# An expert-parallel two-layer network: from unrolled, framework-ordered instructions to one section with hand-set semaphores and a looping TensorE

## The chip, the cores and the metric

The kernel runs on one core of one Trainium2 chip. The metric is device time in microseconds, the median of several runs. Times inside a run come from the hardware profiler's trace, whose span runs from the first to the last instruction of the core.

## The reference

Eight experts, each with 256 rows of 512 values, a hidden width of 2048 and its own two weight matrices:

```python
n_experts, capacity, hidden, expert_hidden = 8, 256, 512, 2048
x  = randn(8, 256, 512);  w1 = randn(8, 512, 2048);  w2 = randn(8, 2048, 512)   # all float32
h   = np.matmul(x, w1)
h   = np.maximum(h, 0)
out = np.matmul(h, w2).astype(np.float32)
```

Each weight matrix of one expert has 4 MB in float32, so w1 and w2 together are 64 MB that are read once. The input x and the output have 4 MB each.

## The kernel before

The weights are loaded by GpSimd's DMA queue, which turns float32 into bf16 on the way. The loads are made for pairs of experts (8 MB a load), and for the last pair one expert at a time, the last w2 in two halves. On the chip there is room for four experts of w1 and four of w2 (two buffers of a pair each). x is loaded into the place of a later w2 pair, transposed by TensorE into xT, and copied out by VectorE and ScalarE in turns.

A first layer (`layer1`) makes 16 column blocks of h, four matmuls each, two blocks to a psum buffer; ScalarE applies the ReLU into hT. A second layer (`layer2`) makes two row blocks of the output, 16 matmuls each. The framework (Tile) sets the semaphores; the order of TensorE's and GpSimd's instructions is that of the program text.

```python
psum_t = ...(name="psum_t", bufs=2)     # transposes
psum_h = ...(name="psum_h", bufs=3)     # first layer
psum_o = ...(name="psum_o", bufs=3)     # second layer
hT_pool = ...(name="hT_pool", bufs=2)

def layer1(e):
    hT = hT_pool.tile([P, K2, C], BF16, name="hT")
    for pr in range(K2 // 2):                          # 8 groups
        h_ps = psum_h.tile([P, 2, C], FP32, name="h_ps")
        for s in range(2):
            j = pr * 2 + s
            for ko in range(K1):                       # 4 matmuls of 256 columns
                nc.tensor.matmul(h_ps[:, s, :], w1_r[:, ko, :, j], xT[:, ko, :, e, :],
                                 start=(ko == 0), stop=(ko == K1 - 1))
        nc.scalar.activation(hT[:, pr*2:pr*2+2, :]..., h_ps[:]..., Relu)
    return hT

def layer2(e, hT):
    # 32 matmuls of 512 columns; order (m, k), for the last expert (k, m)
    ...
            nc.vector.tensor_copy(out_sb[:, e, m, :], o_ps[m][:])
    # last expert: one of its two copies on ScalarE, both into out_last
```

The first layers of a pair come ahead of both second layers, except for the last pair, whose weights are loaded one expert at a time:

```python
for i, g in enumerate(GROUPS):                         # (0,1) (2,3) (4,5) (6,7)
    issue(i + B, i + B)                                # loads whose buffer is free by then
    whole = len(g) > 1 and (g,) in W1_LOADS            # true for the first three pairs
    if whole:
        hs = [layer1(e) for e in g]
        issue(i + 1 + B, i + B)
    else:
        hs = [None] * len(g)
    for e, hT in zip(g, hs):
        layer2(e, hT or layer1(e))
        if e == 5:
            ...; store_first(); ...                    # a small store, then the last half of w2
        if e == E - 2:
            store()                                    # experts 0 to 6, 3.5 MB
nc.sync.dma_start(out_v[:, E - 1, :], out_last[:]...)  # expert 7, 512 KB
```

Of the kernel before, what the change touches and what calls it, by code (L numbers as in the profile page):

```python
# [1 line left out]

# [5 lines left out]

FP32 = mybir.dt.float32  # L10
BF16 = mybir.dt.bfloat16


@with_exitstack
def kernel(
    ctx: ExitStack,
    tc: tile.TileContext,
    x: bass.AP,
    w1: bass.AP,
    w2: bass.AP,  # L20
    out: bass.AP,
):
    nc = tc.nc
    P = 128
    E, C, H = x.shape
    F = w1.shape[2]
    MC = C // P
    K1 = H // P
    K2 = F // P

    R = E * C // P

    x_v = x.rearrange("e (pp r) k -> (e pp) (r k)", r=R)
    w1_v = w1.rearrange("e (p ko) n -> p e (ko n)", ko=K1)
    w2_v = w2.rearrange("e (p j) n -> p e (j n)", p=P)
    out_v = out.rearrange("e (p mo) k -> p e (mo k)", mo=MC)

    GROUPS = [(0, 1), (2, 3), (4, 5), (6, 7)]
    W1_LOADS = [(g,) for g in GROUPS[:-1]] + [((6,),), ((7,),)]
    W2_LOADS = [(g, 0, K2) for g in GROUPS[:-1]] + [((6,), 0, K2), ((7,), 0, 8), ((7,), 8, K2)]
    NG = max(len(g) for g in GROUPS)
    GROUP = {e: g for g in GROUPS for e in g}

    const = ctx.enter_context(tc.tile_pool(name="const", bufs=1))
    w1_pool = ctx.enter_context(tc.tile_pool(name="w1_pool", bufs=4 // NG))  # L50
    w2_pool = ctx.enter_context(tc.tile_pool(name="w2_pool", bufs=4 // NG))
    hT_pool = ctx.enter_context(tc.tile_pool(name="hT_pool", bufs=2))
    psum_t = ctx.enter_context(tc.tile_pool(name="psum_t", bufs=2, space=bass.MemoryType.PSUM))
    psum_h = ctx.enter_context(tc.tile_pool(name="psum_h", bufs=3, space=bass.MemoryType.PSUM))
    psum_o = ctx.enter_context(tc.tile_pool(name="psum_o", bufs=3, space=bass.MemoryType.PSUM))

    identity = const.tile([P, P], BF16, name="identity")
    xT = const.tile([P, K1, MC, E, P], BF16, name="xT")
    out_sb = const.tile([P, E - 1, MC, H], FP32, name="out_sb")
    out_last = const.tile([P, MC, H], FP32, name="out_last")  # L60

    HEAD = 4
    x_head = const.tile([P, HEAD * H], FP32, name="x_head")
    x_sb = w2_pool.tile([P, NG, K2 * H], BF16, name="w2_sb")[:, 0, :]

    w1t, w2t = {}, {}

    def load_x():
        nc.gpsimd.dma_start(x_sb[:, HEAD * H:], x_v[:, HEAD * H:])  # L69

    def load_w1(es):
        g = GROUP[es[0]]
        if es[0] == g[0]:
            w1t[g] = w1_pool.tile([P, NG, K1 * F], BF16, name="w1_sb")
        i = es[0] - g[0]
        nc.gpsimd.dma_start(w1t[g][:, i:i + len(es), :], w1_v[:, es[0]:es[-1] + 1, :])  # L76

    def load_w2(es, a, b):
        g = GROUP[es[0]]
        if es[0] == g[0] and a == 0:  # L80
            w2t[g] = w2_pool.tile([P, NG, K2 * H], BF16, name="w2_sb")
        i = es[0] - g[0]
        nc.gpsimd.dma_start(  # L83
            w2t[g][:, i:i + len(es), a * H:b * H],
            w2_v[:, es[0]:es[-1] + 1, a * H:b * H],
        )

    def store_first():


        nc.gpsimd.dma_start(  # L91
            out_v[:16, 0:5:2, :16], out_sb[:16, 0:5:2, 0, :16]
        )

    def store():
        nc.gpsimd.dma_start(  # L96
            out_v[:, :E - 1, :], out_sb[:].rearrange("p e m h -> p e (m h)")
        )

    def transpose_x():  # L100


        x_r = x_sb.rearrange("p (r2 m q ko) -> p r2 m q ko", m=MC, q=P, ko=K1)
        for i, (ko, m) in enumerate((ko, m) for ko in range(K1) for m in range(MC)):
            ps = psum_t.tile([P, R // MC, P], BF16, name="xt_ps")
            for r2 in range(R // MC):
                nc.tensor.transpose(ps[:, r2, :], x_r[:, r2, m, :, ko], identity[:])  # L107
            src = ps[:].rearrange("k r2 ep -> k ep r2")
            dst = xT[:, ko, m].rearrange("k e (pp r2) -> k (e pp) r2", r2=R // MC)
            if i % 2:  # L110
                nc.scalar.copy(dst, src)  # L111
            else:
                nc.vector.tensor_copy(dst, src)  # L113

    def layer1(e):
        g = GROUP[e]
        w1_r = w1t[g][:, e - g[0], :].rearrange("p (ko q j) -> p ko q j", ko=K1, j=K2)
        hT = hT_pool.tile([P, K2, C], BF16, name="hT")
        for pr in range(K2 // 2):
            h_ps = psum_h.tile([P, 2, C], FP32, name="h_ps")  # L120
            for s in range(2):
                j = pr * 2 + s
                for ko in range(K1):
                    nc.tensor.matmul(  # L124
                        h_ps[:, s, :],
                        w1_r[:, ko, :, j],
                        xT[:, ko, :, e, :],
                        start=(ko == 0),
                        stop=(ko == K1 - 1),
                    )  # L130
            nc.scalar.activation(  # L131
                hT[:, pr * 2:pr * 2 + 2, :].rearrange("p a c -> p (a c)"),
                h_ps[:].rearrange("p a c -> p (a c)"),
                mybir.ActivationFunctionType.Relu,
            )
        return hT

    def layer2(e, hT):
        g = GROUP[e]
        last = e == E - 1  # L140
        o_ps = [psum_o.tile([P, H], FP32, name="o_ps") for _ in range(MC)]
        if last:
            order = [(k, m) for k in range(K2) for m in range(MC)]
        else:
            order = [(k, m) for m in range(MC) for k in range(K2)]
        for k, m in order:
            nc.tensor.matmul(  # L147
                o_ps[m][:],
                hT[:, k, m * P:(m + 1) * P],
                w2t[g][:, e - g[0], k * H:(k + 1) * H],  # L150
                start=(k == 0),
                stop=(k == K2 - 1),
            )
            if k == K2 - 1:
                if last and m == 1:
                    nc.scalar.copy(out_last[:, m, :], o_ps[m][:])  # L156
                elif last:
                    nc.vector.tensor_copy(out_last[:, m, :], o_ps[m][:])  # L158
                else:
                    nc.vector.tensor_copy(out_sb[:, e, m, :], o_ps[m][:])  # L160

    loads = []
    for i, g in enumerate(GROUPS):
        own = [(load_w1, l) for l in W1_LOADS if l[0][0] in g]
        own += [(load_w2, l) for l in W2_LOADS if l[0][0] in g]
        own.sort(key=lambda f: (f[1][0][0], f[0] is load_w2))
        loads += [(i, *f) for f in own]
    tail = loads.pop()  # L170

    def issue(ready1, ready2):

        while loads:
            i, f, l = loads[0]
            if i >= (ready1 if f is load_w1 else ready2):
                break
            loads.pop(0)
            f(*l)

    B = 4 // NG
    nc.sync.dma_start(x_head[:], x_v[:, :HEAD * H])
    nc.vector.tensor_copy(x_sb[:, :HEAD * H], x_head[:])  # L183
    with tc.manual_schedule(engines={mybir.EngineType.PE, mybir.EngineType.Pool}):
        load_x()
        make_identity(nc, identity)
        issue(B, B - 1)
        transpose_x()
        for i, g in enumerate(GROUPS):
            issue(i + B, i + B)  # L190
            whole = len(g) > 1 and (g,) in W1_LOADS
            if whole:
                hs = [layer1(e) for e in g]
                issue(i + 1 + B, i + B)
            else:
                hs = [None] * len(g)
            for e, hT in zip(g, hs):
                layer2(e, hT or layer1(e))
                if e == 5:
                    issue(E, E)  # L200
                    store_first()
                    loads.append(tail)
                    issue(E, E)
                if e == E - 2:
                    store()
    nc.sync.dma_start(out_v[:, E - 1, :], out_last[:].rearrange("p m h -> p (m h)"))

# [1 line left out]
_INS = ['x', 'w1', 'w2']  # L209
# [26 lines left out]
```

## Time and profile before

| | |
|---|---|
| time, median of 3 runs | 181.32 us (181.3 to 181.46) |
| span of the profiled run | 179.7 us, 1827 instructions |
| TensorE busy, matmuls | 127.1 us (71%), 824 |
| ScalarE busy | 44.1 us (25%) |
| VectorE busy | 16.5 us (9%) |
| GpSimd busy | 9.9 us (6%) |
| moved by DMA | 40.48 MB written at the far end, mean 225 GB/s |
| read from HBM | 71.30 MB |
| mean granted TensorE clock | 0.930 |

The page divides the span into 40 slices and gives for each the busy share of every engine in tenths. The chain of work that ended last is followed back from the last instruction, at each step to what released it. "another core or an unknown queue" in it stands for a load whose end the chain could not name; where TensorE waits in that way before a layer, the wait ends with the landing of that layer's weights. Durations of matmuls in the trace overlap, so the time of a layer is read from the start of its first matmul to the start of the next layer. GB/s counts what is written, which for weights is bf16, half of what is read.

### The profile page before, as it was taken

What the parts mean: (1) busy time and instruction counts of PE and PEld (TensorE: products, weight loads), DVE (VectorE), ACT (ScalarE), POOL (GpSimd) and SP (SyncE); (2) the same over time, 40 slices, a digit from 0 to 9 for tenths busy, and PEclk for the clock granted to TensorE, in tenths of its full rate; (3) what the DMA queues carried; (4) which work ended last, traced back from release to release, by engine and by line L of the source; (5) the groups of instructions that cost most, each with busy time, mean ns of one, the idle gap of its engine ahead of it and who ended that gap; (6) DMA issues with size and microseconds to landing.
All of it is one profiled execution on the core that took longest, in us unless ns stands there. A gap on an engine that the chain in (4) does not pass through costs nothing.

```text
span 179.7 us, 1827 instructions
## 1 busy us (share of the span) xinstructions
PE 127.1 (71%) x824; PEld 90.5 (50%) x832; DVE 16.5 (9%) x20; ACT 44.1 (25%) x70; POOL 9.9 (6%) x20
## 2 busy tenths in 40 slices
PE   0017600899629991999569943999199999999960
PEld 0017500699514440899434412999034479469520
DVE  0205500000001111000002210000002210110010
ACT  2004400266500000266500000566100026116210
POOL 7000100000100001000100030000002000002000
PEclk9999975699978999699999997899969999999998
DMA  6999998999999899999999999999999999999995
GB/s 201 252 219 204 233 230 186 226 233 208 201 233 230 190 222 233 208 201 233 230 193 219 233 208 201 233 230 193 219 233 204 204 233 228 195 210 214 349 420 217
DMA packets 3735, 40.48 MB, mean 225 GB/s; under 512 B 272, under 2 KB 272, under 8 KB 1296
## 3 DMA queue, kind: packets, MB, share of 16 engines
q0 software_dynamic: 3440, 38.80, 96.8%
q1 hardware_dynamic: 288, 1.57, 2.4%
q8 instruction: 6, 0.10, 0.2%
q14 instruction: 1, 0.01, 0.0%
HBM read 71.30 MB, written 4.20 MB: 420 GB/s over the span
## 4 chain that ended last, share of the span: by engine, by line
PE 58%; DMA 27%; another core or an unknown queue 9%; POOL 1%; issue 1%; ACT 0%; POOLq 0%
PE o_ps L147 32%; DMA w_sb<-in_w_dram 27%; PE h_ps L124 25%; POOL w_sb L76 0%; POOL w_sb L69 0%; ACT out_last L156 0%; POOL identity masks.py:199 0%; POOL identity masks.py:197 0%; POOLq masks.py:199 0%; POOLq L220 0%
## 5 line engine op out<-in xcount | busy, mean ns | idle before, releaser
L124 PE MATMUL h_ps<-xT,w_sb 128*128 128x256 bf16 x512 | 61.3, 285 | 20.2 <-DMA w_sb<-in_w_dram 20.2
L124 PEld LDWEIGHTS <-w_sb 128*128 128x128 bf16 x512 | 58.3, 146 | 24.1 <-DMA w_sb<-in_w_dram 21.9
L147 PE MATMUL o_ps<-w_sb,hT 128*128 128x512 bf16 x248 | 58.6, 393 | 12.8 <-DMA w_sb<-in_w_dram 12.2
L131 ACT ACTIVATE hT<-h_ps 128x512 bf16<-128x512 f32 x64 | 38.2, 597 | 106.8 <-PE h_ps L124 106.8
L147 PEld LDWEIGHTS <-hT 128*128 128x128 bf16 x256 | 25.6, 101 | 44.3 <-issue 9.3
L160 DVE COPY out_sb<-o_ps 128x512 f32<-128x512 f32 x14 | 9.7, 692 | 128.7 <-PE o_ps L147 128.7
L107 PE MATMUL xt_ps<-identity,w_sb 128*128 128x128 bf16 x64 | 7.7, 309 | 13.8 <-DVE w_sb L183 6.9
L107 PEld LDWEIGHTS <-w_sb 128*128 128x128 bf16 x64 | 6.7, 145 | 14.6 <-DVE w_sb L183 6.9
L111 ACT COPY xT<-xt_ps 128x1024 bf16<-128x1024 bf16 x4 | 4.0, 1012 | 16.5 <-PE xt_ps L107 16.5
L83 POOL DMA_DIRECT2D w_sb<-in_w_dram x6 | 3.8, 637 | 53.6 <-PE o_ps L147 36.5
L113 DVE COPY xT<-xt_ps 128x1024 bf16<-128x1024 bf16 x4 | 4.9, 1224 | 10.2 <-PE xt_ps L107 10.2
L76 POOL DMA_DIRECT2D w_sb<-in_w_dram x5 | 3.3, 658 | 44.6 <-PE h_ps L124 44.6
L96 POOL DMA_DIRECT2D out_dram<-out_sb x1 | 1.0, 968 | 27.3 <-issue 27.3
L91 POOL DMA_DIRECT2D out_dram<-out_sb x1 | 0.6, 554 | 29.2 <-DVE out_sb L160 29.2
L156 ACT COPY out_last<-o_ps 128x512 f32<-128x512 f32 x1 | 0.6, 585 | 6.3 <-PE o_ps L147 6.3
L158 DVE COPY out_last<-o_ps 128x512 f32<-128x512 f32 x1 | 0.7, 692 | 13.4 <-PE o_ps L147 13.4
L183 DVE CAST w_sb<-x_head 128x2048 bf16<-128x2048 f32 x1 | 1.2, 1228 | 5.6 <-DMA x_head<-in_x_dram 5.6
L111 ACT ACT_TABLE_LOAD x1 | 1.3, 1283 | 0.7 <-PEq L220 0.7
L69 POOL DMA_DIRECT2D w_sb<-in_x_dram x1 | 0.7, 679 | 0.8 <-POOLq L220 0.8
masks.py:199 POOL TENSOR_SCALAR_AFFINE_SELECT identity<-identity 128x128 bf16<-128x128 bf16 x1 | 0.3, 287 | 0.1
masks.py:197 POOL MEMSET identity<- 128x128 bf16 x1 | 0.2, 223 | 0.0
L220 POOL MEMSET const-float32-0.0<- 128x1 f32 x1 | 0.1, 93 | 0.2 <-issue 0.2
(3 smaller groups left out, 0.3 us busy)
## 6 DMA issues: line engine op xcount, KB each, us to landing
w_sb<-in_w_dram POOLq DMA_DIRECT2D x6, 4096.0 KB, 62.1
w_sb<-in_w_dram POOLq DMA_DIRECT2D x3, 2048.0 KB, 51.5
out_dram<-out_sb POOLq DMA_DIRECT2D x1, 3584.0 KB, 12.9
w_sb<-in_w_dram POOLq DMA_DIRECT2D x2, 1024.0 KB, 44.7
w_sb<-in_x_dram POOLq DMA_DIRECT2D x1, 1536.0 KB, 11.6
x_head<-in_x_dram SPq DMA_DIRECT2D x1, 1024.0 KB, 4.8
out_dram<-out_last SPq DMA_DIRECT2D x1, 512.0 KB, 4.3
out_dram<-out_sb POOLq DMA_DIRECT2D x1, 3.0 KB, 27.8
```

Of the source, the lines that this page charges most:

```text
L69: nc.gpsimd.dma_start(x_sb[:, HEAD * H:], x_v[:, HEAD * H:])
L76: nc.gpsimd.dma_start(w1t[g][:, i:i + len(es), :], w1_v[:, es[0]:es[-1] + 1, :])
L83: nc.gpsimd.dma_start(w2t[g][:, i:i + len(es), a * H:b * H], w2_v[:, es[0]:es[-1] + 1, a * H:b * H],)
L96: nc.gpsimd.dma_start(out_v[:, :E - 1, :], out_sb[:].rearrange("p e m h -> p e (m h)"))
L107: nc.tensor.transpose(ps[:, r2, :], x_r[:, r2, m, :, ko], identity[:])
L111: nc.scalar.copy(dst, src)
L113: nc.vector.tensor_copy(dst, src)
L124: nc.tensor.matmul(h_ps[:, s, :], w1_r[:, ko, :, j], xT[:, ko, :, e, :], start=(ko == 0), stop=(ko == K1 - 1),)
L131: nc.scalar.activation(hT[:, pr * 2:pr * 2 + 2, :].rearrange("p a c -> p (a c)"), h_ps[:].rearrange("p a c -> p (a c)"), mybir.ActivationF ...
L147: nc.tensor.matmul(o_ps[m][:], hT[:, k, m * P:(m + 1) * P], w2t[g][:, e - g[0], k * H:(k + 1) * H], start=(k == 0), stop=(k == K2 - 1),)
L160: nc.vector.tensor_copy(out_sb[:, e, m, :], o_ps[m][:])
L183: nc.vector.tensor_copy(x_sb[:, :HEAD * H], x_head[:])
```

## The change

All of the work goes into one section in which each engine has its own program text, and every wait is a semaphore set by hand. TensorE's program becomes loops: one over the four values of ko for the transposes, one over the experts, and inside it one over blocks of four column blocks of F. The addresses of weights and xT come from registers there. The aim is a short TensorE program whose order and waits are all explicit.

The parts that matter, with cuts marked by "...":

```diff
-    psum_h = ctx.enter_context(tc.tile_pool(name="psum_h", bufs=3, space=bass.MemoryType.PSUM))
-    psum_o = ctx.enter_context(tc.tile_pool(name="psum_o", bufs=3, space=bass.MemoryType.PSUM))
+    NS = 4
+    GJ = 2
+    UG = 2
+    NG = K2 // GJ
...
+    w1_sb = nc.alloc_sbuf_tensor("w1_sb", [P, NS, K1 * F], BF16)
+    w2_sb = nc.alloc_sbuf_tensor("w2_sb", [P, NS, K2 * H], BF16)
+    hT = nc.alloc_sbuf_tensor("hT", [P, K2, C], BF16)
+    h_ps = [nc.alloc_psum_tensor(f"h_ps{i}", [P, GJ * C], FP32) for i in range(UG)]
+    o_ps = [nc.alloc_psum_tensor(f"o_ps{i}", [P, H], FP32) for i in range(MC)]
...
+    with tc.tile_critical(no_gpsimd_drain=True):
+        sp = nc.sync
...
+        for i, (w, e, n, a, b) in enumerate(loads):       # same loads, same order
+            sp.wait_ge(d_w[i], 16)
+            if w == 1:
+                sp.sem_inc(c_w1, n)
             else:
+                sp.sem_inc(c_w2, 2 * n * b // K2)
...
+        for i, (w, e, n, a, b) in enumerate(loads):       # GpSimd
+            old = e + n - 1 - NS
+            if w == 2 and e == 2:
+                pool.wait_ge(p_xt, K1 * MC)
+            if old >= 0:
+                if w == 1:
+                    pool.wait_ge(p_h, NG * (old + 1))
+                else:
+                    pool.wait_ge(p_o, MC * (old + 1))
...
+            for g in range(NG):                           # ScalarE, for each e
+                act.wait_ge(p_h, e * NG + g + 1)
+                act.activation(hT[...], h_ps[g % UG][:], Relu).then_inc(c_h)
...
+        def take(s, n):
+            pe.wait_ge(s, n).then_inc(s, -n)
...
+        with nc.Fori(0, E, 1, engines=[PE]) as e:
+            ring = pe.snap((e % NS) * (K1 * F))
+            col = pe.snap(e * P)
+            take(c_w1, 1)
+            with nc.Fori(0, NG // UG, 1, engines=[PE]) as u:
+                first = pe.snap(ring + u * (UG * GJ))
+                for g in range(UG):
+                    take(c_h, 1)
+                    for i in range(GJ):
+                        for ko in range(K1):
+                            c = first + (ko * F + g * GJ + i)
+                            mm = pe.matmul(
+                                h_ps[g][:, i * C:(i + 1) * C],
+                                w1_f[:, bass.DynSlice(c, P, step=K2)],
+                                xT[:, ko, :, bass.ds(col, P)],
+                                start=(ko == 0), stop=(ko == K1 - 1),
+                            )
+                    mm.then_inc(p_h)
+            take(c_o, MC)
+            for k in range(K2):
+                if k % (K2 // 2) == 0:
+                    take(c_w2, 1)
+                late = k - (K2 - UG * GJ)
+                if late >= 0 and late % GJ == 0:
+                    pe.wait_ge(c_h, late // GJ + 1)
+                for m in range(MC):
+                    mm = pe.matmul(
+                        o_ps[m][:], hT[:, k, m * P:(m + 1) * P],
+                        w2_f[:, bass.ds(ring + k * H, H)],
+                        start=(k == 0), stop=(k == K2 - 1),
+                    )
+                    if k == K2 - 1:
+                        mm.then_inc(p_o)
```

A `take` waits until a semaphore has a value and lowers it by that much. Sync waits for each load and passes the news on to TensorE by raising `c_w1` or `c_w2`. There is one hT, so ScalarE waits for the second layer of expert e - 1 before the first ReLU of expert e. The two copies of the last expert and its store stay as they were; the small store and the 3.5 MB store are issued by GpSimd at the same places of its queue.

## The prediction

> **What bounds the kernel now.** I read three views of the kernel before: the DMA row and queue table of the page, then the chain of work that ended last, then stretches of the span cut at the points where the chain changes hands. The first says that the transfers are saturated from start to end.
>
> ```profile
> DMA  6999998999999899999999999999999999999995
> q0 software_dynamic: 3440, 38.80, 96.8%
> ```
>
> Forty slices at 9, one queue with 96.8% of the time of 16 engines: no rearrangement of waits can make the 64 MB of weights come sooner. What it can spoil is the end. The chain shows who follows whom in the second half:
>
> ```profile
> 105.30 5.32 another core or an unknown queue
> 110.62 0.05 issue
> 110.66 15.56 PE h_ps L124 x128
> 126.22 3.76 another core or an unknown queue
> 129.98 0.05 issue
> 130.03 0.39 PE o_ps L147
> ...
> 142.95 2.75 PE o_ps L147 x12
> 145.70 6.99 PE h_ps L124 x64
> 152.69 0.21 PE o_ps L147
> ...
> 166.96 0.43 PE o_ps L147 x2
> 167.39 0.05 issue
> 167.44 6.44 PE o_ps L147 x29
> 173.88 0.02 issue
> 173.90 0.58 ACT out_last L156
> ```
>
> Columns are start, duration, what. TensorE waits for a load until 110.66 (w1 of experts 4 and 5), does both first layers in one go (128 matmuls, 15.56 us), waits for the w2 of the pair until 130.03, and from there to 173.88 has hardly a gap. So the transfers set everything up to 130.0 and TensorE sets the rest: after 130.0 come two second layers (15.7 us for the pair 4 and 5), then first and second layer of expert 6 and of expert 7. The loads land 19.3 us apart for each 8 MB (52.6, 71.95, 91.3, 110.66, 130.0 in the chain), 434 GB/s. The last views give the unit costs, columns being the stretch, its length, then busy time and instruction counts by engine, the granted clock, DMA share and GB/s:
>
> ```profile
> 52.60:56.10 3.50, 3.26 (x9) 1.28 (x10) 0.00 (x0) 0.00 (x0) 0.00 (x0) 0.58 1.05 225
> 159.70:166.80 7.10, 7.05 (x65) 7.05 (x66) 0.62 (x1) 4.18 (x7) 0.97 (x1) 1.00 1.03 215
> 166.80:173.90 7.10, 7.01 (x33) 3.04 (x31) 0.21 (x1) 0.60 (x1) 0.00 (x0) 1.00 1.00 392
> ```
>
> A first layer is 64 matmuls in 7.2 us (112 ns for one matmul and its weight load), a second layer 32 matmuls in about 6.95 us (216 ns each; the out_sb copies of L160 lie 3.46 us apart, 16 matmuls). After a wait of several us the clock is low for 3.5 us (0.58 in the first row): 9 matmuls in 3.5 us where 16 would fit, a loss of 1.5 us, and the pair at 130.0 takes 15.7 where two layers make 13.9, a loss of 1.8; I use 1.6. From the last matmul (173.87) to the end of the span (179.7) are 5.8 us: copy 0.6, then the store of the last expert, 4.3 from issue to landing, which shares the engines with the 3.5 MB store (392 GB/s in the last row), and the closing waits.
>
> [...]
>
> **The change part by part.**
> Loads: same order, sizes and queue, and the same buffers (four slots of w1 and of w2). Their issue moves later because slots come free later, but the queue is deep enough: the load of w1 for 4 and 5 was issued at 48.0 and did not start to move before 91.3. In the new order its release, the first layer of expert 1, comes at about 70. The last piece of w2 needs the copy of expert 4, about 137 to 140, and its turn comes at about 164. So I leave all arrivals where they are: w2 of 4 and 5 at 130.0.
> Waits: sync now forwards each load through a second semaphore[...]; only the load at 130.0 counts.
> Scalar and Vector: same instructions and sizes (64 of 597 ns, 14 of 692 ns). Psum buffers for h go from 3 to 2. A group of 8 matmuls takes 0.9 us; its ReLU starts 0.29 us after the last matmul ends (160.65 by eight times 112 ns, 160.94 in the timeline), takes 0.60 and must be seen by TensorE: the buffer is free about 1.0 to 1.2 us later, the other buffer covers 0.9. A stall of 0.1 to 0.3 us per group, about 1.3 us per first layer, if issue is not slower than that anyway.
> Order on TensorE: this is the part I am surest of. Before, both first layers of a pair were done before its w2 landed. The loop does first and second layer of each expert in turn, so at 130.0 the first layer of 5 is still to come. After 130.0 there are 4 second layers and 3 first ones: 4 x 6.95 + 3 x 7.2 = 49.4, plus 1.6 for the cold clock = 51.0, so TensorE ends at 181.0 instead of 173.9, even if loops and waits are free.
> Loop and register addresses: each matmul pair of the first layer needs a register operation for its weight address, then a load and a matmul whose addresses come from registers. [...] So I reckon 10.4 us net for a first layer where it was 7.2, and 6.95 for a second.
> Check of the middle: w2 of 2 and 3 lands at 91.3; 6.95 + 1.6 + 10.4 + 6.95 + 10.4 brings the first layer of 4 to 127.6, just before 130.0. So the sum from 130.0 holds: 4 x 6.95 + 3 x 10.4 + 1.6 = 60.6, TensorE ends at 190.6. The end is then a copy, and a store alone on the DMA: the big store needs expert 6 only and runs beside the layers of expert 7, so I take 5.2 instead of 5.8. Span 195.8; the times before lie 1.6 above the span (181.3 against 179.7). Sum: 197.4, I say 197.
>
> **The rivals.**
> A: loops are free (issue hides in TensorE's queue), only the order costs: 181.0 + 5.2 + 1.6 = 187.8. For it: 7.2 us first layers at 1.00 clock leave the sequencer no visible gap now. Against: weight addresses change at every load.
> B: issue isn't the limit but two psum buffers are: first layers of 8.5, 3 x 1.3 more: 191.7.
> C: issue is far slower[...]: first layers of 14. Then the load at 130.0 no longer matters; from 52.6 on TensorE never waits: 52.6 + 1.6 + 8 x 6.95 + 7 x 14 = 207.8, and 6.8 on top: 214.6. [...]
> D: the DMA hides it all, the time stays at 181 or falls, since hand-set waits cut some latency. The 40 slices at 9 speak against any gain: before 130.0 nothing but arrivals counts, and after it the DMA ends at about 177.5 while TensorE alone asks for 181.0.
>
> **Range and chances.** A is the lower edge, C nearly the upper: 188 to 213, skewed to the slow side because the cost of register-addressed issue isn't in any trace here and multiplies by 64 pairs and three to seven layers. Same (up to 184.9) would need TensorE to do seven layers in 48 us, less than the sum of their present times: 0.03. Faster by 2%, 177.7, would lie below what saturated transfers and their closing take: 0.01. Slower: 0.96.
>
> **What would show it.** In the trace after: arrivals at 52, 91 and 130 as now; seven layers in a row after 130.0; the first layer's length against 7.2, 8.5, 10.4 or 14; inside it, whether TensorE idles at the start of each group (psum), at each second group (the loop turn), or evenly between pairs (register operations); the DMA row falling off in the last slices while TensorE works. I am wrong if arrivals move (a load issued too late), if first layers come out at 7.2[...].

## The result and the profile after

| | before | after |
|---|---|---|
| time, median | 181.44 us (6 runs) | 203.43 us (6 runs) |
| ratio | | 1.119, 95% interval 1.116 to 1.123 |
| span of the profiled run | 179.7 us | 201.6 us |
| instructions in the span | 1827 | 2844 |

The first view is the page of the changed kernel again: the DMA row of 40 slices, and the queue that carries the loads.

```profile
DMA  6949999999999999999999999999999998019602
q0 software_dynamic: 3440, 38.80, 86.6%
```

Two things are new: a hole in the third slice (about 10 to 15 us), and an end that falls apart. The same 38.80 MB now fill 86.6% of a longer span. Where TensorE sets the end, the timeline of the changed kernel shows it; columns are start, busy time, engine, line, operation, count, and in brackets the idle time ahead of the group and what ended it:

```profile
13.58 2.36 PE L206 MATMUL xt_ps<-identity,w_sb 128*128 128x128 bf16 x16 [13.58 <-PEq L196]
...
132.93 8.76 PE L246 MATMUL o_ps<-w_sb,hT 128*128 x32 [2.47 <-PEq L196]
141.53 1.91 PE L229 MATMUL h_ps<-xT,w_sb 128*128 x16
143.77 2.46 PE L229 MATMUL h_ps<-xT,w_sb 128*128 x16 [0.33 <-issue]
146.81 2.48 PE L229 MATMUL h_ps<-xT,w_sb 128*128 x16 [0.57 <-PEq L196]
149.85 2.48 PE L229 MATMUL h_ps<-xT,w_sb 128*128 x16 [0.57 <-PEq L196]
152.71 7.08 PE L246 MATMUL o_ps<-w_sb,hT 128*128 x32 [0.38 <-PEq L196]
...
188.90 7.08 PE L246 MATMUL o_ps<-w_sb,hT 128*128 x32 [0.38 <-PEq L196]
```

The last wait for a load ends at 132.93, and from there TensorE does seven layers in a row: the second layer of expert 4, then first and second of 5, 6 and 7. A first layer lasts from 141.53 to 152.71, 11.18 us. It comes in four bursts of 16 matmuls, one for each turn of the inner loop, with 0.33 to 0.57 us of idle time ahead of the second to fourth, and the later bursts follow each other about every 3.05 us. The first burst is faster (2.24 us to the next): it was issued while TensorE still worked through the second layer ahead of it (the branch that closes this turn is a record at 141.22, ahead of the turn's first matmul at 141.53). The idle time is put down to PEq, TensorE's own sequencer, or to issue. A `take` that waits for another engine counts as PEq too (the 1.41 us between two second layers further down are such a wait), so this alone does not exclude ScalarE; the trace does, for the third and fourth turn. Their first takes run at 146.38 and 149.43, and the ReLUs that free those buffers have ended 0.67 us earlier (145.71 and 148.77). Only the first take of the second turn, at 143.30, comes straight after its ReLU (143.26). A second layer lasts 6.92 us (152.71 to 159.63, where the next first layer starts), as before.

The hole early on belongs to GpSimd. The first view is of the changed kernel, with the issue of the first weight loads:

```profile
2.23 0.30 POOL masks.py:199 TENSOR_SCALAR_AFFINE_SELECT identity<-identity 128x128 bf16<-128x128 bf16 x1
13.62 2.18 POOL L133 DMA_DIRECT2D w_sb<-in_w_dram  x3 [11.09 <-issue]
```

and this is the same kernel's stretches there (length, busy time by engine, clock, DMA share, GB/s):

```profile
10.00:12.00 2.00, 0.00 (x0) 0.00 (x0) 0.00 (x0) 0.00 (x0) 0.00 (x0) 1.00 0.93 197
12.00:13.00 1.00, 0.00 (x0) 0.00 (x0) 0.00 (x0) 0.00 (x0) 0.00 (x0) 1.00 0.02 0
13.00:14.00 1.00, 0.42 (x4) 0.37 (x4) 0.00 (x0) 0.00 (x0) 0.38 (x1) 1.00 0.00 0
14.00:15.00 1.00, 1.00 (x9) 0.76 (x7) 0.19 (x1) 0.00 (x0) 1.00 (x2) 1.00 0.00 0
```

GpSimd has finished the identity at 2.53, but in the trace its `drain` stands from 1.60 to 13.09, and the first weight load follows at 13.62. The transfer of x has ended by then (DMA share 0.02 from 12 on; issued at 1.45, it lands 11.5 us later by the page). The issue then takes time, and for some 3 us nothing is moved. In the kernel before the three loads were issued from 2.45 us on.

So the 22 us have four candidates: the order of the layers, the drain, the loops with their register addresses, and the smaller costs of the hand-set section (two psum buffers, the end of the section).

### The profile page after: what moved, and what is told of

It reads as the page before. It is cut to its first block, busy times and chain, and to the rows that moved or that the text cites. A ratio compares the mean times of both kernels' runs of the same rounds, so it can differ in the third digit from the quotient of the medians.

```text
span 201.6 us, 2844 instructions
## 1 busy us (share of the span) xinstructions
PE 145.6 (72%) x832; PEld 98.7 (49%) x832; DVE 15.9 (8%) x21; ACT 44.1 (22%) x70; POOL 9.7 (5%) x19
## 3 DMA queue, kind: packets, MB, share of 16 engines
q0 software_dynamic: 3440, 38.80, 86.6%
## 5 line engine op out<-in xcount | busy, mean ns | idle before, releaser
L229 PE MATMUL h_ps<-xT,w_sb 128*128 x512 | 76.0, 298 | 23.7 <-PEq L196 21.6
L229 PEld LDWEIGHTS h_ps<-xT,w_sb 128*128 x512 | 65.9, 145 | 34.8 <-issue 28.5
L246 PE MATMUL o_ps<-w_sb,hT 128*128 x256 | 61.3, 401 | 11.7 <-PEq L196 11.7
L246 PEld LDWEIGHTS o_ps<-w_sb,hT 128*128 128x128 bf16 x256 | 25.6, 103 | 45.0 <-issue 19.3
L206 PE MATMUL xt_ps<-identity,w_sb 128*128 128x128 bf16 x64 | 9.4, 294 | 14.9 <-PEq L196 14.9
L206 PEld LDWEIGHTS xt_ps<-identity,w_sb 128*128 x64 | 7.3, 113 | 16.9 <-issue 16.1
L189 ACT COPY out_sb<-o_ps 128x512 f32<-128x512 f32 x1 | 0.6, 585 | 6.9 <-PE o_ps L246 6.9
## 6 DMA issues: line engine op xcount, KB each, us to landing
w_sb<-in_x_dram POOLq DMA_DIRECT2D x1, 1536.0 KB, 11.5
```

What stands on the lines that cost most here:

```text
L189: act.copy(out_sb[:, E - 1, 1, :], o_ps[1][:]).then_inc(v_last)
L206: t = pe.transpose(xt_ps[m][:, r2, :], x_r[:, r2, m, bass.DynSlice(ko, P, step=K1)], identity[:],)
L229: mm = pe.matmul(h_ps[g][:, i * C:(i + 1) * C], w1_f[:, bass.DynSlice(c, P, step=K2)], xT[:, ko, :, bass.ds(col, P)], start=(ko == 0), sto ...
L246: mm = pe.matmul(o_ps[m][:], hT[:, k, m * P:(m + 1) * P], w2_f[:, bass.ds(ring + k * H, H)], start=(k == 0), stop=(k == K2 - 1),)
```

## Experiments

Every run is timed against the kernel before on the same chip (181.4 in each comparison).

**Drain away.** The identity's own instruction raises the semaphore.

```diff
-        make_identity(nc, identity[:], nomemset=True)
-        pool.drain().then_inc(s_ident)
+        pool.affine_select(
+            out=identity[:], in_=identity[:], compare_op=mybir.AluOpType.not_equal,
+            fill=1.0, base=0, pattern=[[-1, P]], channel_multiplier=1,
+        ).then_inc(s_ident)
```

> The changed kernel, but GpSimd's drain after the identity is gone: the identity's own instruction raises the semaphore. Theory (the drain waits for the x transfer, so the first weight loads are issued at 13.6 us, the queue runs dry and every later arrival is 2.9 us late): first weight load issued before 4 us, w2 of experts 4 and 5 lands at 130.0 instead of 132.9, time 203.4 - 2.9 = 200.5. Rival (arrivals are late because sync passes each load on through a second semaphore): arrivals and time stay, 203.4.

Measured 199.9 us, 1.103 of before (1.099 to 1.107). Timeline of this kernel:

```profile
2.46 2.18 POOL L135 DMA_DIRECT2D w_sb<-in_w_dram  x3
...
129.49 8.77 PE L248 MATMUL o_ps<-w_sb,hT 128*128 x32 [2.91 <-PEq L198]
```

The loads are issued at 2.46, and the second layer of expert 4 starts at 129.49 instead of 132.93. The time fell by 3.5 us. Arrivals are now even a little ahead of the kernel before (130.03), so the extra semaphore hop through sync costs nothing that can be seen here.

**Order alone.** The kernel before with one line changed: every expert does first and second layer in turn.

```diff
-            whole = len(g) > 1 and (g,) in W1_LOADS
+            whole = False
```

> The kernel before, fully unrolled and with the framework's semaphores, but first and second layer of each expert in turn, as in the change. Theory (order alone leaves seven layers after 130.0): TensorE ends at 181.0, time 187.8. Rival (the loads decide, order is worth nothing): 181.4.

Measured 187.02 us, 1.030 (1.028 to 1.032). Chain of work of this kernel, start, duration, what:

```profile
120.59 9.29 another core or an unknown queue
129.88 0.05 issue
129.92 9.63 PE o_ps L147 x32
139.55 6.99 PE h_ps L124 x64
146.54 6.91 PE o_ps L147 x32
...
174.32 6.92 PE o_ps L147 x32
181.24 0.02 issue
181.27 0.59 ACT out_last L156
```

TensorE waits 9.3 us for w2 of experts 4 and 5 with a first layer still undone, and then ends at 181.24: the order costs 5.6 us in time with no loop, no register and no hand-set semaphore in it. The end is 4.2 us behind the last matmul instead of 5.8, because the last store has the DMA engines for itself (2.7 us from issue to landing by its page, 4.3 in the kernel before).

**Loops unrolled.** All addresses of the two layers static; order, semaphores, psum buffers and drain as in the change.

```diff
-        with nc.Fori(0, E, 1, engines=[PE]) as e:
-            ring = pe.snap((e % NS) * (K1 * F))
-            col = pe.snap(e * P)
+        for e in range(E):
+            ring = (e % NS) * (K1 * F)
+            col = e * P
...
-            with nc.Fori(0, NG // UG, 1, engines=[PE]) as u:
-                first = pe.snap(ring + u * (UG * GJ))
+            for u in range(NG // UG):
+                first = ring + u * (UG * GJ)
```

> The changed kernel with both TensorE loops over experts and blocks unrolled, so that all addresses of its two layers are static; order, hand-set semaphores, two psum buffers and the drain stay. Theory (loop turns and register operations make up all of the longer first layer): first layer 7.2 instead of 11.2, three of them after the last wait, time 203.4 - 3 x 4.0 = 191.4. Rival (two psum buffers or hand-set waits hold it): first layer 8.2 to 8.5, time 194.5 to 195.

Measured 193.17 us, 1.065 (1.063 to 1.067). Chain:

```profile
133.50 8.39 PE o_ps L246 x32
141.88 7.35 PE h_ps L229 x64
149.23 6.91 PE o_ps L246 x32
```

A first layer takes 7.35 us: 3.83 of the 4.19 us that it had gained are gone. The 0.36 that is left against the 6.99 of the order-only kernel is neither of the two expected values.

**Inner loop alone unrolled** (the second pair of lines of the diff above; the loop over experts and one register operation ahead of each weight load stay).

> The changed kernel with only the inner loop over blocks unrolled: the loop over experts and one register operation for each weight load stay. Theory (each pair is paced by its register operation at 144 ns, the turns cost 0.74 us each on top): first layer about 9.0, time 203.4 - 3 x 2.2 = 196.8. Rival 1 (the turn is all of it): 7.2 and 191.4. Rival 2 (registers are all of it): 10.5 to 11.2 and 201 to 203.

Measured 197.87 us, 1.090 (1.088 to 1.092). Chain:

```profile
142.46 1.75 PE h_ps L229 x16
144.20 0.11 issue
144.31 7.00 PE h_ps L229 x48
151.31 0.09 issue
151.40 7.07 PE o_ps L246 x32
```

A first layer takes about 9.1 us, and in it 48 matmuls take 7.00: 146 ns each, where the unrolled one has 7.35 / 64 = 115. The first 16 take 109 ns each, from the backlog of the second layer. The 146 ns are a mean of two things, which the trace of the changed kernel shows singly, in the same stretch of program. Late in a turn, weight loads start 124 ns apart there, with the register operation as a record of 46 ns between two of them; every eighth time, where the `take` for the next psum buffer stands, it is 275 ns (147.80 to 148.07), 0.15 us more. It looked as if the register operations cost 1.8 us a layer and the turns 2.1 on top. The next run shows that this is only half right.

**Loop kept, addresses static.** The loop over experts is unrolled, the loop over blocks stays, and every turn computes the same four column blocks. Three quarters of h are left out, so only the time is read.

```diff
-                first = pe.snap(ring + u * (UG * GJ))
+                first = ring
```

> The loop over blocks stays, the loop over experts is unrolled, and all addresses are static: each of the four turns computes the same four column blocks, so three quarters of h are left out (repeated). Theory (a turn costs its 0.69 us whatever the addresses): first layer 7.35 + 3 x 0.69 = 9.4, time 193.2 + 3 x 2.07 = 199.4. Rival (static pairs are issued faster than TensorE works them off, so the turn hides behind the queue): 7.4 to 8, time 193 to 195.

Measured 192.86 us, 1.062 (1.058 to 1.065): as fast as the unrolled kernel. Chain:

```profile
156.97 0.05 issue
157.03 1.03 PE o_ps L246 x4
158.05 7.35 PE h_ps L229 x64
```

The 64 matmuls run through four turns in 7.35 us without a gap that the profile shows. My theory of a turn with a price of its own fell. A turn takes time in the sequencer (its taken compare-and-branch is a record of 0.21 us in the trace of the changed kernel), but with static pairs none of it shows. The changed kernel's trace has both sides. The branch that closes the first turn of a layer runs at 141.22, 0.31 us before the first matmul of that turn, and what ends last ahead of the second turn is a ReLU (143.26), not the branch. The branch that closes the second turn runs at 146.03, 0.13 us after that turn's last weight load has started, and the next matmul starts only at 146.81. There the register operations have used up the sequencer's lead, and only then does a turn show. That the lead is what hides the turns with static pairs is read from these two places and the 7.35 us.

**Which part of a register address costs.** Two kernels take the operation away and keep the register. In one, a loop of two turns has four experts written out in each: weight addresses are static, the address of xT is a register written once an expert.

```diff
-        with nc.Fori(0, E, 1, engines=[PE]) as e:
+        with nc.Fori(0, E // NS, 1, engines=[PE]) as half:
+            for q in range(NS):
...
-            ring = pe.snap((e % NS) * (K1 * F))
-            col = pe.snap(e * P)
+                ring = q * (K1 * F)
+                col = pe.snap(half * (NS * P) + q * P)
```

> The changed kernel with a loop of two turns over halves of the experts, four experts and all blocks written out in each turn: weight addresses are static, the address of xT still comes from a register, written once for each expert. Theory (a pair is slowed by the register operation ahead of it, not by reading an address from a register): first layer 7.35 as in the unrolled one, time 193.2. Rival (a register address itself slows the matmul): first layer 9.1, time 197.9.

In the other, with only the inner loop unrolled as above, all 64 matmuls of a layer load one weight block, its address in a register that stays as it is. The other blocks are left out, so only the time is read.

```diff
-                            c = first + (ko * F + g * GJ + i)
+                            c = ring
```

> The variant with only the inner loop unrolled (loop over experts kept), but all 64 matmuls of a first layer load the same weight block, at an address read from a register that no operation rewrites between pairs. It leaves out the other weight blocks, so only its time is read. Theory (the register operation ahead of each weight load is what paces the pairs): first layer 7.35, time 193.2. Rival (a weight load whose address is in a register is slow by itself): 9.1 and 197.9.

Measured 193.37 (1.064, 1.061 to 1.068) and 193.41 us (1.064, 1.062 to 1.067). The first layer is 7.35 in the chain of the first. In the timeline of the second, a first layer starts at 157.39 and the next second layer at 164.73, 7.34 later:

```profile
157.39 7.50 PE L228 MATMUL h_ps<-xT,w_sb 128*128 x64
164.73 7.07 PE L245 MATMUL o_ps<-w_sb,hT 128*128 x32
```

Reading an address from a register costs nothing that these runs show, neither for the matmul nor for its weight load. The operation that computes it costs: 7.35 with none between the pairs, 9.1 with about one a pair, 11.2 with about one a pair and loop turns. That the edit took it away shows in the instruction counts of the pages: 2716 with the inner loop unrolled, 2236 here, 60 fewer for each of eight first layers of 64 pairs.

**Three psum buffers** for h in the unrolled kernel instead of two.

```diff
-    h_ps = [... for i in range(UG)]
+    h_ps = [... for i in range(NB)]          # NB = 3, used in turns
```

> The unrolled variant with three psum buffers for h instead of two, nothing else. Theory (two buffers are the 0.36 us by which its first layer is longer than that of the kernel before, 7.35 against 6.99): first layer 7.0, time 193.2 - 3 x 0.36 = 192.1. Rival (the hand-set waits cost it, as they stand as instructions of their own): 7.35 and 193.2.

Measured 192.0 us, 1.057 (1.055 to 1.060). Chain:

```profile
150.20 6.85 PE o_ps L247 x31
157.06 6.99 PE h_ps L230 x64
```

6.99 again: the 0.36 came from having two buffers and not three, and hand-set waits cost TensorE nothing inside a layer. The lengths of the layers carry this; the times of the kernel with two buffers alone spread from 192.1 to 193.8.

**Hand-set semaphores alone.** Unrolled, no drain, first layers of a pair ahead of its second layers (two hT buffers).

```diff
...
+        for e in range(0, E - 2, 2):
+            layer1(e)
+            layer1(e + 1)
+            layer2(e)
+            layer2(e + 1)
+        for e in (E - 2, E - 1):
+            layer1(e)
+            layer2(e)
```

> Hand-set semaphores alone: TensorE fully unrolled, no drain on GpSimd, first layers of a pair ahead of its second layers as in the kernel before (two hT buffers), two psum buffers. Theory (order, drain, loop turns and register operations are all that cost; 0.36 for each of two first layers after 130.0 and a closing that is about 1 us longer remain): 183. Rival 1 (hand-set semaphores are as good as the framework's): 181.4. Rival 2 (they save latency): 180 or less.

Measured 183.23 us, 1.009 (1.007 to 1.012). Its timeline has a gap that I had not foreseen:

```profile
130.90 6.85 PE L251 MATMUL o_ps<-w_sb,hT 128*128 128x512 bf16 x31 [2.44 <-PEq L198]
139.16 7.07 PE L251 MATMUL o_ps<-w_sb,hT 128*128 128x512 bf16 x31 [1.41 <-PEq L198]
```

Two second layers in a row need two pairs of output buffers; there is one pair here, and both fill up at the same time, so TensorE waits 1.41 us between them.

**The same with more psum:** three buffers for h, four for the output, two of which the transposes borrow.

```diff
-    h_ps = [... for i in range(UG)]
-    o_ps = [... for i in range(MC)]
+    h_ps = [... for i in range(NB)]          # NB = 3
+    o_ps = [... for i in range(2 * MC)]
```

> Hand-set semaphores alone, with three psum buffers for h and four for the output (the transposes borrow two of these). Theory (the gap of 1.41 us between the two second layers of a pair is the copy of the only two output buffers, and 0.36 a first layer is the missing third h buffer): the gap gone, first layers 7.0, TensorE ends near 173.5; a closing about 1 us longer than in the kernel before remains: 182.2. Rival 1 (the transfers and stores set the end anyway): 183.2 as without it. Rival 2 (it beats the kernel before): below 181.3.

**And as a loop of two turns** with static weight addresses, so that TensorE's program is half as long as the unrolled one, with four buffers for h, and with the first layers of experts 2 and 3 no longer taken together:

```diff
+        with nc.Fori(0, E // NS, 1, engines=[PE]) as half:
+            layer1(0, half)
+            layer1(1, half)
+            layer2(0)
+            layer2(1)
+            for q in range(2, NS):
+                layer1(q, half)
+                layer2(q)
```

> The same with a TensorE loop of two turns, four experts written out in each, static weight addresses and one register for the address of xT, four psum buffers for h, first layers of experts 0 and 1 and of 4 and 5 ahead of their second layers. Theory (a loop without register operations between its matmuls is free): the same time as the unrolled one, 182.2, within 0.5. [...]

Measured 183.16 us (1.009, 1.007 to 1.011) and 183.23 us (1.010, 1.008 to 1.011). The turn back of the looped one falls between experts 3 and 4, and the timeline has no idle time there: from the second layer of expert 3 to the first layer of expert 4 pass 6.91 us, as long as any second layer.

```profile
107.67 7.07 PE L254 MATMUL o_ps<-w_sb,hT 128*128 128x512 bf16 x32
114.58 14.14 PE L234 MATMUL h_ps<-xT,w_sb 128*128 x128
...
174.50 0.35 SPq L103 DMA_DIRECT2D out_dram<-out_sb  x1
```

Neither gained on the 183.23 of the kernel with the gap, though the gap is gone and first layers are back at 7.0. In the profiled run of the unrolled one the pair of second layers after the last wait took 16.75 us (130.19 to 146.94), where the kernel with the gap needed 15.17 (130.90 to 146.07) and the looped one 13.81 (130.38 to 144.19), and with that the gain was gone; the mean granted clocks of the three runs were 0.922, 0.951 and 0.934. The looped one issues its last store 1.2 us earlier than the kernel with the gap, at 174.50 and not 175.71, and still gains nothing. The reason shows in the DMA issues of the pages (KB, us from issue to landing), first of the kernel with the gap, then of the looped one, then of the kernel before:

```profile
out_dram<-out_sb SPq DMA_DIRECT2D x1, 512.0 KB, 3.6
out_dram<-out_sb SPq DMA_DIRECT2D x1, 512.0 KB, 4.6
out_dram<-out_last SPq DMA_DIRECT2D x1, 512.0 KB, 4.3
```

The last store shares the engines with the 3.5 MB store (DMA share 1.03 from 175 to 177 in the looped kernel), and lands at 179.3, 179.1 and 178.8. The transfers set this end, as the first rival of the unrolled kernel had it, and a microsecond of TensorE more or less does not move it. That the theory for the kernel with the gap came out at 183 was therefore in part luck: its 0.36 for each first layer were not on the path that ended last.

What is left comes after the last landing: 2.4 us in the looped kernel (span 181.5), 0.9 in the kernel before (179.7). Sync's waits for the other engines there (us in total, times, longest) are longer, again looped kernel and kernel before:

```profile
SPq L297 <- PEq L297: 1.7, 2, 1.1
SPq L231 <- PEq L231: 0.6, 2, 0.4
```

The trace of the changed kernel, whose end is as long (2.4 us after the last landing at 199.25, these waits 1.6, 2, 1.0), says what they wait for. GpSimd has a `drain` at the end of the program there, from 199.62 to 200.74, after the handshake that ends the section. In the kernel before GpSimd reaches that drain at 164.71, with the issue of the 3.5 MB store, and is through at 178.24, before the last store has landed. So by estimate 1.1 of the 1.8 us are this drain, taken to be as long in the looped kernel, and 0.3 the later landing; no run was made without the drain. All three versions are about 1% slower, which is little but clear of the scatter (the lowest edge of the intervals is 1.007): no version with a hand-set section came down to the kernel before.

The sum, each step from its run: order 5.6, drain 3.5, loops with register operations 203.4 - 193.2 = 10.2, the missing psum buffer 193.2 - 192.0 = 1.2, closing of the section, with all else that is left of it, 183.2 - 181.4 = 1.8. Together 22.3, against 22.0 measured. The steps were taken from different kernels, so the agreement is a check and no proof that they add.

## Why the prediction was right, and where not

The time, 203.4, lies in the range, 6.4 above the point. Step by step:

- **Order of layers**: right. Seven layers after the last wait; alone it was predicted at 187.8 and measured 187.0, with TensorE ending at 181.2 for 181.0. Hitting it so closely was luck in part. The 7.2 us for a first layer were read from a line of the chain; from first matmul to next layer, as all other layers are read, the two late ones of the kernel before have 6.98 and 7.05, and alone they have 6.99. The layer after the wait cost more than the 1.6 us for the cold clock: 9.63 with the order alone, 2.7 more than 6.91, and 8.60 in the changed kernel, 1.7 more, with a granted clock of 0.54 over the first 3.7 us and 1.00 after them. (Not every wait of several us was followed by a low clock: in the kernel before, TensorE idled for 3.49 us up to 91.31, and the next 3.5 us have 1.00.) The errors in these lengths cancel in large part.
- **Arrivals**: this step failed. I wrote that loads are only issued later and arrive the same, and looked only at the loads that wait for a free slot. I passed over the drain between x and the first weight load, which lasted until the x transfer had landed (13.09 and 13.00 us); it moved the last arrival to 132.9, 2.9 of the 6.4 us. Moved arrivals were one of the prediction's own signs of being wrong, though it expected them from a slot that comes free too late. (The DMA row that it starts from has 36 nines in 40 slices, not forty; the argument doesn't depend on it.)
- **First layer**: 10.4 predicted, 11.18 measured, 3 x 0.78 = 2.3 us. The 10.4 was the author's estimate: no trace before showed what a register operation, a take or a loop turn takes, so that it came within 0.8 us is luck. The changed kernel's own terms are 124 ns for most pairs, 7.9 us for 64 of them; about 3.05 - 16 x 0.124 = 1.07 us for a turn with its two takes, slower first pairs included, 4.3 for four; and about 1.0 less for the lead from the second layer. Of a turn's 1.07 us the compare-and-branch lasts 0.21.
- **Turns and register operations as a sum**, as the expectations for the two runs with one loop opened had them: wrong in kind. A turn cost nothing with static pairs (7.35 us in four turns and in none), and no take cost anything with static pairs and three psum buffers (6.99); both cost once register operations had taken the sequencer's lead (11.18). The lead that a second layer leaves is seen in the first burst of each first layer, where 16 pairs take 109 ns each.
- **End**: 5.2 predicted, 195.8 to 201.6 is 5.8 measured. The lone store is faster, 2.6 us instead of 4.3 by the DMA issues of the page, but the end of the section takes that back.
- **Rivals**: A (loops free) failed for this loop, and holds for a loop without register operations. B (psum, 1.3 us a layer by an estimate from the 0.29 and 0.60 us of a ReLU in the trace) is real but small, 0.36 a layer with static pairs; in the changed kernel only one take in a first layer, at the second turn, still comes straight after the ReLU that it needs. C, whose 14 us no trace backed, fell: first layers took 11.18, and the longest branch of TensorE in the trace of the changed kernel lasts 0.23 us. D fell: 203.4, not 181.

The sum with measured terms is 132.9 + 8.6 + 3 x 11.18 + 3 x 6.92 = 195.8, where the prediction had 190.6: 2.9 from the drain, 2.3 from the layers.

## What to carry to other kernels

In a loop on TensorE, look at what stands between two matmuls: a register operation for every weight address paced the pairs here (124 ns against 109) and then exposed each wait and each loop turn too (11.18 us a first layer against 7.35), while registers written once an expert, and a loop body long enough to keep weight addresses static, cost nothing in these runs (7.35). When TensorE sets the end, count the layers that remain after the last load lands; rolling a loop up may change that order (5.6 us here). Before replacing a framework's waits, check what a drain on the engine that issues loads waits for (3.5 us here).

## What the runs showed of the hardware that was not expected

- A GpSimd drain with a transfer of its queue under way lasted 11.5 us, until 0.1 us after that transfer had landed; removing it gave 3.5 us. A drain that began 0.4 us after the last transfer had landed, at the end of the changed kernel, still lasted 1.1 us.
- A taken loop turn on TensorE was invisible with static addresses (7.35 us for 64 matmuls in four turns and in none), though its compare-and-branch lasts 0.21 us in the trace of the changed kernel. A turn back over a body with half of all expert layers left no idle time either (6.91 us for the second layer ahead of it).
- One register operation ahead of a weight load took a pair from 109 to 124 ns, and a take every eight pairs, not seen with static addresses and three psum buffers, then added 0.15 us. Reading an address from a register took nothing (7.35 and 7.34 us a first layer).
